# The third mixer with GpSimd's part given to TensorE, ScalarE and VectorE, and a run-time exchange of the fullest expert

## The chip, the core and the metric

The program runs on one core of one Trainium2 chip. The metric is the device time of one execution in microseconds: the median of three runs, and beside it one profiled execution with its trace. Engines: PE is TensorE (PEld its weight loads), DVE VectorE, ACT ScalarE, POOL GpSimd, SP SyncE, which issues most DMAs. Every engine takes its instructions in program order.

## What is computed

A batch of one with 256 positions of 1024 channels passes a first block (feed-forward layers, a short convolution, an mLSTM) and then a second block, with which the change deals:

```python
def second_block(...):
    h = layer_norm_2(x, ln_in_g, ln_in_b)          # right behind first_block's own last layer norm
    y = mixer_sublayer(h, ...)                     # the "third mixer"
    h = layer_norm_2(DEEPNORM_ALPHA_2 * h + y, ln1_g, ln1_b)
    e = (p @ ple_proj) * sigmoid(h @ ple_gate)
    m = moe_ffn(h, w_router, router_bias, exp_w_up, exp_w_down)   # 16 experts, 2 for each position
    return layer_norm_2(DEEPNORM_ALPHA_2 * h + m + e, ln2_g, ln2_b)

def mixer_sublayer(h, ...):
    u_pool, u_conv, c_q, c_kv, k_r, g_logits = split(h @ w_in)
    gates = sigmoid(g_logits + b_gate)
    y_pool = pool_mixer(u_pool) @ pool_proj        # causal mean over 2, 4, 8, 16 positions less u, then 4 small products
    y_conv = conv_module(u_conv) @ conv_proj       # depthwise convolution of width 31 on 512 channels, layer norm, silu
    y_mla = mla(c_q, c_kv, k_r) @ mla_proj         # 8 heads, softmax over allowed keys
    return (gates[0] * y_pool + gates[1] * y_conv + gates[2] * y_mla) @ w_out
```

Everything is float32. A weight matrix is used as a pair: `wh`, rounded to the fast matmul type fp32r, and `wl = raw - wh`; three matmuls (h·wh, l·wh, h·wl) stand for one product. A matmul on plain fp32 operands needs no pair.

## The kernel before

The 256 positions lie in two tiles t = 0, 1 of 128 partitions (`X_72`, `X_73` in the order listings below), or, transposed, channels on partitions and 256 positions along a row. `first()` runs the first block up to 1034 us; its instructions are the same after the change. `second()` follows:

- **Boundary.** While the last feed-forward's down products end (`g.tail`), DVE norms each tile twice: `ln_math` with the first block's gain and bias `gb`, then again with the second block's (`yp` in the listings). Each norm is statistics (L637, L639, L619), POOL's `rs_r` (L621), then four DVE operations on halves of 512 (L644 subtract mean and multiply gain, L645 multiply `rs_r` and add bias). TensorE turns the tile by transposes (L657), ACT rounds it to `xh` (L660), DVE makes `xl` (L664). `m2_head(t)` then projects tile t.
- **m2_body.** `conv_in` and the attention's input product, the pool products `pool_mm` (L1376), the attention's norms and transposes (`cTh`, `cTl`), queries (`uq`, L1312 turns them), keys, values. Then three merges in the order pool, attention, convolution (`MERGE`), each a gate product (L583 to L585), a projection, and DVE's multiply and add (L1578, L1580). Between a merge's blocks stand steps of the softmax (`mla`: scores L1420, exponent L1431, norm L1438 and L1440, turn L1455, output L1466) and of the convolution (`tap`).
- **pool_mean** runs on POOL: some 30 operations (L1393 to L1399) for the four windows; DVE splits the result into `yp` (L569).
- **conv31.** Channel groups 0 to 2 of four take 30 taps each on DVE (L1501 `cz`); group 3 takes 30 on ACT and POOL: ACT scales a shifted row into `tap` (L1493), POOL adds it (L1494). Tables (`TAPS_...`) say how many taps follow each block.
- **Weight pairs** of this part come through a ring (`st`): SP loads `raw`, ACT rounds it to `wh` (L298), and DVE or POOL makes `wl` (L299). Tables (`PUMP_...`) say which; POOL makes 21 between 1034 and 1340 us.
- **Routing** (1300 to 1345 us) is a chain of small DVE operations. It picks the fullest expert, and from it one run-time number, the row of its weights; 32 positions beyond an expert's 64 slots go through a spill round that needs the fullest expert's six weight tiles a second time (`SPILL`).
- **moe.** 16 experts in a fixed order (`_expert(i)`), six tiles of 1 MB each, in all 108 tiles with six for the spill round and six for gate and projection. SP issues the loads as slots come free; in the loop's last step (e = 15) the spill round runs beside expert 15. `combine` adds the results, `last_ln` norms and stores them.

Of the kernel before, what the change touches and what calls it, by code (L numbers as in the profile page):

```python
# [8 lines left out]
F32 = mybir.dt.float32  # L9
# [6 lines left out]
P = 128  # L16
# [29 lines left out]
def _pieces():  # L46
# [68 lines left out]
    def pl(j):  # L115
        add(("pl", j), 1024, "w_in_2", lambda w: _cols(w[0], j * P))
# [36 lines left out]
TAPS_POOL = "1011112302111112", "2020233020033323"  # L153
TAPS_MLA = "1111111010202032", "2300320331230300"
PUMP_POOL = "1210"
PUMP_MERGE = "13100221", "10112311", "10013123"
TAPS_CONV = "2020121032020130", "1030200011320012"
# [12 lines left out]
N_TILES = 108  # L170
SPILL = 16
# [4 lines left out]
def _wtile(e, j):  # L176
    e = 15 if e == SPILL else 16 if e == 15 else e
    return 6 * e + j + (6 if e >= GATE_AT else 3)


WTILES = {_wtile(e, j): (e, j) for e in range(17) for j in range(6)}
# [67 lines left out]
class Stream:  # L249
    def __init__(self, k, ws):  # L250
# [17 lines left out]
        self.raw, self.hl = {}, {}  # L268
# [21 lines left out]
    def split(self):  # L290
        i = self.nsplit
        r = self.slot(i)[0]
# [6 lines left out]
        self.eng.tensor_sub(l[:, :n], src, h[:, :n])  # L299
        self.hl[i] = (h, l)  # L300
        self.nsplit += 1

# [11 lines left out]
    def get(self, key):  # L314
        i = self.index[key]
        while self.nsplit <= i:
            assert self.slot(self.nsplit)[1] < self.free, key
            self.split()
# [35 lines left out]
def _const():  # L354
# [13 lines left out]
    return c  # L368

# [115 lines left out]
class Kernel:  # L485
# [142 lines left out]
    def ln_steps(self, t, accs, scale, eps, gb=None):  # L628
# [538 lines left out]

    def m2_open(self):
# [9 lines left out]
        self.cs = [x.rearrange("p a n -> p (a n)") for x in (self.tp, self.sg)]  # L1178

# [29 lines left out]
    def trig(self, p):  # L1209
        nc = self.nc  # L1210
        pi = p.tile([P, T], I32, name="pu0")
        pos = self.a["pos"]
        nc.gpsimd.dma_start(pi, bass.AP(tensor=pos.tensor, offset=pos.offset, ap=[[0, P], [1, T]]))
        ang = p.tile([P, T], F32, name="pu1")
        n = p.tile([P, T], F32, name="pu2")
# [13 lines left out]
    def m2_body(self):  # L1229
# [3 lines left out]
        self.qf = p0.tile([P, 8, T], F32, name="qf")  # L1233
        self.kf = p0.tile([P, 8, T], F32, name="kf")
        self.vv = [p0.tile([P, 512], F32, name=f"vv{t}") for t in range(2)]
# [4 lines left out]
        self.bcast(qg, a["rowp"][776:1416])  # L1240
        self.rot = p.tile([P, 2, T], F32, name="rot")
        self.cos, self.sin = self.rot[:, 0], self.rot[:, 1]
        self.trig(p)
# [15 lines left out]
        junk = p.tile([P, 384], F32, name="pm0")  # L1259
# [13 lines left out]
        next(cin, None)  # L1273
        self.taps = self.conv31()
        self.yp = self.m2.tile([P, 2, 4, T], F32R, name="yp")
        u = [self.pool_mm(p, j) for j in range(2)]
# [8 lines left out]
        u += [self.pool_mm(p, 2)]  # L1285
# [13 lines left out]
        u += [self.pool_mm(p, 3)]  # L1299
        for j in range(4):  # L1300
            self.pool_mean(p, j, u[j])
# [941 lines left out]
```

## Time and profile before

| | us |
|---|---|
| median of three runs (lowest, highest) | 1604.82 (1602.35, 1605.71) |
| the profiled execution's own time | 1610.17 |
| its span, first to last instruction | 1608.4 |
| PE busy | 1517.4 (94%) |
| DVE busy | 922.0 (57%) |
| ACT busy | 637.4 (40%) |
| POOL busy | 157.6 (10%) |

Busy shares are averages over stages that have different limits. Rows name a line of the kernel, an engine, an operation, and output<-input. A wait is the idle time of an engine ahead of an instruction, with what released it. The granted clock is the share of full speed that TensorE was given; 1.00 stands for 2.4 GHz.

### The profile page before, as it was taken

Reading aid. Unit: us, or ns where it says so; the run is one execution under the profiler, and the core shown is the slowest. Engines: PE = TensorE matmul, PEld = TensorE weight load, DVE = VectorE, ACT = ScalarE, POOL = GpSimd, SP = SyncE. Lnnn points to the kernel's source line nnn. Section 1 sums busy time; section 2 is a strip of 40 time slices with the busy share of each in tenths; the row PEclk is TensorE's granted clock in tenths of the full one; section 3 lists DMA queues with packets and bytes.
Section 4 is the critical chain, followed back from the end, with each engine's and each line's share of the span. In section 5 each row is a group of like instructions: output and inputs, shape, how many; then the busy total and the mean of one; then the engine's idle time right before and its main releaser. Section 6 shows DMA issues by size and latency. Waiting matters only on the chain.

```text
span 1608.4 us, 23409 instructions
## 1 busy us (share of the span) xinstructions
PE 1517.4 (94%) x9667; PEld 1249.1 (78%) x9668; DVE 922.0 (57%) x1367; ACT 637.4 (40%) x998; POOL 157.6 (10%) x161
## 2 busy tenths in 40 slices
PE   7999999899999999999999999979797999999986
PEld 5999989779999899988777999858687974434432
DVE  5654567575456755577667455577899564222223
ACT  4544435444443544435524444416663431111111
POOL 1000000000000000010000000133675200000001
PEclk9999999999999999999999999989898999999998
DMA  6655546354554654535325555325416666999993
GB/s 253 236 210 183 184 145 221 132 208 163 206 184 145 238 178 180 187 138 221 131 105 209 184 184 184 135 115 205 142 53 240 227 253 262 407 370 415 417 417 157
DMA packets 57391, 338.68 MB, mean 211 GB/s; under 512 B 6464, under 2 KB 6768, under 8 KB 25536
## 3 DMA queue, kind: packets, MB, share of 16 engines
q1 hardware_dynamic: 55008, 325.97, 54.0%
q0 software_dynamic: 1696, 8.96, 1.5%
q10 hardware_dynamic: 576, 2.22, 0.4%
q8 instruction: 77, 1.26, 0.3%
q14 instruction: 34, 0.28, 0.1%
HBM read 336.07 MB, written 1.05 MB: 210 GB/s over the span
## 4 chain that ended last, share of the span: by engine, by line
PE 73%; DVE 15%; issue 4%; DMA 3%; ACT 3%; POOL 1%; DVEq 0%; SPq 0%; ACTq 0%; POOLq 0%
PE mm L583 11%; PE mm L584 11%; PE mm L585 11%; PE mm L1914 7%; PE acc L573 6%; PE acc L574 6%; PE acc L575 6%; DVE wl L299 4%; PE mm L1937 3%; DVE cz L1501 3%; DMA raw<-in_ws_dram 2%; ACT wh L298 1%; DMA wh<-in_we_dram 1%; PE mm L1883 1%; DVE X L644 1%
## 5 line engine op out<-in xcount | busy, mean ns | idle before, releaser
L299 DVE TENSOR_TENSOR wl<-raw,wh 128x1024 fp32r<-128x1024 f32 (+1 forms) x381 | 458.8, 1244 | 117.9 <-ACT wh L298 117.8
L583 PE MATMUL mm<-xh,wh 128*128 128x256 f32 x1640 | 465.0, 284 | 0.0
L298 ACT CAST wh<-raw 128x1024 fp32r<-128x1024 f32 (+1 forms) x404 | 403.3, 1043 | 149.7 <-PE acc L575 57.5
L584 PE MATMUL mm<-xl,wh 128*128 128x256 f32 x1640 | 462.4, 282 | 0.0
L585 PE MATMUL mm<-xh,wl 128*128 128x256 f32 x1640 | 461.8, 282 | 0.0
L583 PEld LDWEIGHTS mm<-xh,wh 128*128 128x128 f32 x1640 | 311.5, 190 | 5.2 <-issue 2.7
L584 PEld LDWEIGHTS mm<-xl,wh 128*128 128x128 f32 x1640 | 310.9, 190 | 2.2
L585 PEld LDWEIGHTS mm<-xh,wl 128*128 128x128 f32 x1640 | 311.3, 190 | 0.0
L393 DVE TENSOR_TENSOR fm<-fs,mm 128x256 f32<-128x256 f32 x80 | 33.7, 422 | 209.5 <-ACT fs L391 209.5
L391 ACT ACTIVATE fs<-mm 128x256 f32<-128x256 f32 x80 | 30.8, 386 | 294.3 <-PE mm L585 294.3
L575 PE MATMUL acc<-wh,fhl 128*128 128x512 f32 x352 | 140.0, 398 | 4.9 <-DVE fhl L569 4.9
L573 PE MATMUL acc<-wh,fhh 128*128 128x512 f32 x352 | 141.1, 401 | 3.3 <-ACT fhh L568 3.3
L574 PE MATMUL acc<-wl,fhh 128*128 128x512 f32 x352 | 140.5, 399 | 0.0
L621 POOL TENSOR_TENSOR rs_r<-rs_v,nhalf 128x1 f32<-128x1 f32 (+2 forms) x22 | 18.3, 830 | 1102.3 <-DVE rs_v L619 1062.5
L575 PEld LDWEIGHTS acc<-wh,fhl 128*128 128x128 f32 x352 | 67.0, 190 | 22.7 <-DVE fhl L569 7.0
L573 PEld LDWEIGHTS acc<-wh,fhh 128*128 128x128 f32 x352 | 67.0, 190 | 18.3 <-ACT fhh L568 5.5
L574 PEld LDWEIGHTS acc<-wl,fhh 128*128 128x128 f32 x352 | 66.9, 190 | 12.6
L299 POOL TENSOR_TENSOR wl<-raw,wh 128x1024 fp32r<-128x1024 f32 (+1 forms) x23 | 58.8, 2567 | 69.0 <-ACT wh L298 69.0
L1501 DVE SCALAR_TENSOR_TENSOR cz<-cz,par 128x256 f32<-128x256 f32 x90 | 65.3, 787 | 0.0
L569 DVE TENSOR_TENSOR fhl<-fm,fhh 128x256 fp32r<-128x256 f32 x80 | 34.1, 426 | 37.8 <-ACT fhh L568 37.8
L1918 ACT ACTIVATE es<-mm 128x256 f32<-128x256 f32 x16 | 6.2, 384 | 117.8 <-PE mm L1914 117.8
L602 PE MATMUL mm<-wh,xh 128*128 128x512 f32 x128 | 45.3, 438 | 4.1 <-ACT xh L660 2.5
(574 smaller groups left out, 2147.6 us busy)
## 6 DMA issues: line engine op xcount, KB each, us to landing
raw<-in_ws_dram SPq DMA_DIRECT2D x197, 1024.0 KB, 4.9
wh<-in_we_dram SPq DMA_DIRECT2D x61, 512.0 KB, 11.3
wl<-in_we_dram SPq DMA_DIRECT2D x61, 512.0 KB, 11.3
w<-in_we_dram SPq DMA_DIRECT2D x23, 1024.0 KB, 12.3
raw<-in_we_dram SPq DMA_DIRECT2D x18, 1024.0 KB, 11.3
gb<-in_lnp_dram POOLq DMA_DIRECT2D x5, 1024.0 KB, 5.1
raw<-in_ws_dram SPq DMA_DIRECT2D x3, 768.0 KB, 4.9
w<-in_wg_dram SPq DMA_DIRECT2D x2, 1024.0 KB, 8.7
```

The source lines that it names most:

```text
L298: self.nc.scalar.copy(h[:, :n], src)
L299: self.eng.tensor_sub(l[:, :n], src, h[:, :n])
L573: mm(out, lh, rh, start=first, stop=False)
L574: mm(out, lh, rl, start=False, stop=False)
L575: mm(out, ll, rh, start=False, stop=last)
L583: mm(out, h[:, c], xh[:, k, s], start=k == 0, stop=False)
L584: mm(out, h[:, c], xl[:, k, s], start=False, stop=False)
L585: mm(out, l[:, c], xh[:, k, s], start=False, stop=k == kn - 1)
L602: mm(ps, self.xh[:, kk, s], h[:, c], start=kk == 0, stop=False)
L1501: nc.vector.scalar_tensor_tensor(o, cz[:, j, d:d + T], dw[j][:, d:d + 1], o, op0=OP.mult, op1=OP.add)
L1914: nc.tensor.matmul(ps[64 * b:64 * b + 64], x, w[:, c:c + 512], start=d == 0, stop=d == KT - 1)
L1937: self.nc.tensor.matmul((pb if i else pa)[64 * i:64 * i + 64], hT[:, a, 64 * b:64 * b + 64], w[:, c:c + 512], start=k == 0, stop=k == 3)
```

## The change

It changes seven things in `second()` and behind it. Line numbers below are the changed kernel's.

1. **Boundary.** The second norm no longer writes a finished tile on DVE. `ln_in` takes the statistics, and ACT normalises the tile in two operations of 512. `in_T` transposes that, and 16 ACT operations of 128x128 apply gain and bias, which lie along partitions now: 8 write `xh`, 8 write the same in fp32 (`y32`, buffer `cz`). `in_low` makes `xl` on DVE. `in_gain` applies gain and bias to the tile itself by four DVE operations of 128x1024, behind both heads.
2. **Weight pairs.** All `wl` are made on DVE but one at the boundary; the tables of POOL's share are gone.
3. **pool_mm and pool_mean.** The pool product is made with positions on partitions, 48 matmuls of 512 columns (before 96 of 256). The mean less u is a product with a constant band matrix: three fp32 matmuls (128, 16 and 128 columns) for each window. The matrix comes by one DMA.
4. **conv31.** Group 3: ACT scales the identity by one tap (128x128, `tap<-ident`), TensorE multiplies the shifted rows by that diagonal (fp32, 256 columns), four taps or six gathering in PSUM, and DVE adds the sum. 30 ACT operations, 30 matmuls, 8 DVE additions.
5. **Softmax.** A reciprocal on DVE and four ACT scalings in each of four steps replace POOL's power and products.
6. **The experts' order.** The fullest expert outside the four that are fixed at the front changes places with the last. The spill round uses the last expert's tiles, so its six own are gone (`N_TILES` 108 to 102). Twelve rows of weights are read by SP from `r_sel` at run time (before one), and routing has 15 more DVE operations (`swap` and others).
7. **The spill round's steps** in the last step move: down products of expert 14 first, spill's gate and up, transposes of 15, then behind the loop spill's transposes, down of 15, spill's down, the outputs.

```diff
 def second(self, g, acc, fs, fe):
-        self.slab_eng, self.slab_pumps, self.slab_ahead = nc.gpsimd, 4, 0
+        self.slab_eng, self.slab_pumps, self.slab_ahead = nc.vector, 4, 2
         self.ln_math(0, acc[0], fs, fe)
-        g.tail(range(NF - LAST2, NF - LAST2 + 2), "pp")
-        self.ln_math(0, None, 0, EPS, self.gb2)
-        g.tail(range(NF - LAST2 + 2, NF), "vpvp")
-        self.ln_pair((acc[1], fs, fe), [(None, 0, EPS, self.gb2)])
+        g.tail(range(NF - LAST2, NF - LAST2 + 2), "")
+        for _ in range(2):
+            st.cast()
+        self.ln_in(0)
+        st.low()
+        g.tail(range(NF - LAST2 + 2, NF), "")
...
+        ln = self.ln_steps(1, acc[1], fs, fe)
+        next(ln)
+        self.in_T(0)
+        next(ln)
+        self.in_low(0)
...
+        self.ln_in(1)
+        st.low()
         self.m2_head(0)
-        self.ln_T(1)
+        self.in_T(1)
+        self.in_low(1)
         self.m2_head(1)
+        self.in_gain()
         self.m2_body()
+    def ln_in(self, t):
...
+        for s in range(2):
+            xs = x[:, s * 512:(s + 1) * 512]
+            nc.scalar.activation(xs, xs, AF.Identity, scale=r, bias=mv[:, 0:1])
+    def in_T(self, t):
...
+        for y in (self.xh[:, :, t * P:(t + 1) * P], self.y32[:, t].rearrange("p (k n) -> p k n", k=KT)):
+            for k in range(KT):
+                nc.scalar.activation(y[:, k], pts[k // 4][:, k % 4 * P:(k % 4 + 1) * P], AF.Identity,
+                                     scale=g[:, k:k + 1], bias=b[:, k:k + 1])
+    def pool_mean(self, j, u):
...
+        mm(ps[:, P:T], u[1][:, c], b[:, BAND:], start=True, stop=False)
+        mm(ps[:, P:BAND], u[0][:, c], b[:, P:BAND], start=False, stop=False)
+        mm(ps[:, :P], u[0][:, c], b[:, :P], start=False, stop=True)
+        self.split(self.yp[:, 0, j], self.yp[:, 1, j], ps[:, :T])
 def norm(x):
-            nc.gpsimd.tensor_tensor(sm, sm, neg, op=OP.pow)
+            nc.vector.reciprocal(sm, sm)
             for b, g in enumerate(gs):
-                nc.gpsimd.tensor_tensor(pr[g], pr[g], sm[:, b, :, None].to_broadcast([P, n, P * (t + 1)]), op=OP.mult)
+                for i in range(n):
+                    nc.scalar.activation(pr[g][:, i], pr[g][:, i], AF.Identity, scale=sm[:, b, i:i + 1])
 def side():
-            for d in range(30):
-                tap = self.tp[:, d % 2]
-                nc.scalar.activation(tap, cz[:, 3, d:d + T], AF.Identity, scale=dw[3][:, d:d + 1])
-                nc.gpsimd.tensor_tensor(o, o, tap, op=OP.add)
+            for d0 in range(0, 30, 4):
+                n = min(4, 30 - d0)
+                for i in range(n):
+                    nc.scalar.activation(dg[:, i], self.ident, AF.Identity, scale=dw[3][:, d0 + i:d0 + i + 1])
                 yield
+                ps = self.acc()
+                for i in range(n):
+                    nc.tensor.matmul(ps[:, :T], dg[:, i], cz[:, 3, d0 + i:d0 + i + T], start=i == 0, stop=i == n - 1)
+                nc.vector.tensor_tensor(o, o, ps[:, :T], op=OP.add)
+                yield
-N_TILES = 108
-SPILL = 16
+N_TILES = 102
+FIXED = 4
+LAST_E = 7
 def wsrc(self, i):
-        if e < SPILL:
+        if e < FIXED:
             r = (6 * _expert(e) + j) * P
             return a["we"][r:r + P]
...
+        return a["we"][bass.ds(self.row * (6 * P) + j * P, P)]
```

Three places in the order of instructions, of the kernel before and of the changed one apart.

VectorE at the boundary, before: the first tile `X_72` from its first norm (gain and bias in `gb`) to the end of the second (in `yp`).

```order
L644 SCALAR_TENSOR_TENSOR X_72<-X_72,ln_mv,gb 128x512
L645 SCALAR_TENSOR_TENSOR X_72<-X_72,rs_r,gb 128x512
L637 BN_STATS ln_st<-X_72 128x6 x2
L639 BN_AGGR ln_mv<-ln_st 128x2
L619 TENSOR_SCALAR rs_v<-ln_mv 128x1
L644 SCALAR_TENSOR_TENSOR X_72<-X_72,ln_mv,yp 128x512
L645 SCALAR_TENSOR_TENSOR X_72<-X_72,rs_r,yp 128x512
L644 SCALAR_TENSOR_TENSOR X_72<-X_72,ln_mv,yp 128x512
L645 SCALAR_TENSOR_TENSOR X_72<-X_72,rs_r,yp 128x512
L299 TENSOR_TENSOR wl_10126<-raw,wh_10125 128x1024
```

VectorE at the same place, after.

```order
L666 SCALAR_TENSOR_TENSOR X_72<-X_72,ln_mv,gb 128x512
L667 SCALAR_TENSOR_TENSOR X_72<-X_72,rs_r,gb 128x512
L1195 BN_STATS ln_st<-X_72 128x6 x2
L1197 BN_AGGR ln_mv<-ln_st 128x2
L641 TENSOR_SCALAR rs_v<-ln_mv 128x1
L1199 SCALAR_TENSOR_TENSOR ln_mv<-ln_mv,rs_r 128x1
L305 TENSOR_TENSOR wl_10100<-raw,wh_10099 128x1024
L305 TENSOR_TENSOR wl_10103<-raw,wh_10102 128x1024
L657 SCALAR_TENSOR_TENSOR X_73<-acc,X_73 128x512 x2
```

The four operations of 512 behind the statistics have left DVE's queue; one small operation and two `wl` stand there, and the second tile's first norm comes sooner.

VectorE from the attention's queries to the first merge, before: `cz` are taps of the convolution's groups 0 to 2, `yp<-pu` splits POOL's means, `yp<-acc,par` the pool products.

```order
L299 TENSOR_TENSOR wl_10939<-raw,wh_10938 128x1024
L1501 SCALAR_TENSOR_TENSOR cz<-cz,par 128x256 x6
L569 TENSOR_TENSOR yp<-pu_10611,yp 128x256
L569 TENSOR_TENSOR yp<-pu_10649,yp 128x256
L569 TENSOR_TENSOR yp<-pu_10707,yp 128x256
L569 TENSOR_TENSOR yp<-krep_10753,yp 128x256
L299 TENSOR_TENSOR wl_11009<-raw,wh_11008 128x1024
L1501 SCALAR_TENSOR_TENSOR cz<-cz,par 128x256 x3
L1350 SCALAR_TENSOR_TENSOR yp<-acc,par,yp 128x256 x2
```

VectorE at the same place, after.

```order
L591 TENSOR_TENSOR yp<-acc,yp 128x256
L305 TENSOR_TENSOR wl_10900<-raw,wh_10899 128x1024
L305 TENSOR_TENSOR wl_10930<-raw,wh_10929 128x1024
L1572 SCALAR_TENSOR_TENSOR cz<-cz,par 128x256 x6
L305 TENSOR_TENSOR wl_10962<-raw,wh_10961 128x1024
L305 TENSOR_TENSOR wl_10991<-raw,wh_10990 128x1024
L1572 SCALAR_TENSOR_TENSOR cz<-cz,par 128x256 x3
L1565 TENSOR_TENSOR cz<-cz,acc 128x256
L1420 SCALAR_TENSOR_TENSOR yp<-acc,par,yp 128x256 x2
```

More `wl` stand in DVE's queue, the splits of the means come singly and earlier and from PSUM, and an addition `cz<-cz,acc` of the diagonals' sum is new.

VectorE at routing's end, before: `r_cnt` is what SP reads at run time, `xg` the first experts' gathered input.

```order
L1860 TENSOR_SCALAR r_cb<-r_cb 128x16
L1861 TENSOR_SCALAR r_cf<-r_cb 128x16
L1862 TENSOR_REDUCE r_cf<-r_cf 128x1
L1864 CAST r_cnt<-r_cf 1x18
L1886 COPY xg_12910<-mm_12901 128x512
L1886 COPY xg_12932<-mm_12923 128x512
```

VectorE at routing's end, after. The number that SP reads, `r_sel`, is made four instructions ahead of the first of these; `r_rv` and `r_wv` are the exchanged columns.

```order
L1974 TENSOR_TENSOR r_aff<-r_m_12860,r_oh 128x32
L1975 TENSOR_TENSOR r_rk<-r_rk,r_aff 128x32
L1976 COPY r_rk<-r_rv 128x2
L1971 TENSOR_TENSOR r_aff<-r_wt,r_oh 128x32
L1972 TENSOR_REDUCE r_wv<-r_aff 128x2
L1973 TENSOR_TENSOR r_m_12868<-r_wt,r_wv 128x2
L1974 TENSOR_TENSOR r_aff<-r_m_12868,r_oh 128x32
L1975 TENSOR_TENSOR r_wt<-r_wt,r_aff 128x32
L1976 COPY r_wt<-r_wv 128x2
L1964 TENSOR_SCALAR r_rv<-r_rv 128x2
L1998 COPY xg_12904<-mm_12895 128x512
L1998 COPY xg_12926<-mm_12917 128x512
```

Thirteen small operations (these ten and three ahead of them) stand between `r_sel` and the `xg` copies that stood right behind `r_cnt`; two more stand ahead of `r_sel`.

## Rows read from the trace of the kernel before

**Rows 1.** Windows: busy time (instructions) of each engine, granted clock, DMA share, GB/s.

```profile
1046.60:1085.00 38.40, 27.39 (x105) 21.39 (x106) 29.38 (x39) 6.01 (x9) 14.44 (x11) 0.82 0.30 114
1120.00:1255.00 135.00, 110.26 (x803) 105.04 (x801) 123.62 (x174) 74.92 (x143) 85.18 (x87) 0.89 0.41 145
1346.00:1564.00 218.00, 217.88 (x1090) 89.80 (x1086) 50.93 (x106) 32.78 (x58) 2.69 (x6) 1.00 0.99 399
```

**Rows 2.** TensorE's waits from 1034 to 1120 us: total, times, longest.

```profile
PE acc L657 <- DVE X L645: 11.1, 4, 4.3
PE acc L1289 <- DVE cTl L569: 1.6, 1, 1.6
```

**Rows 3.** TensorE's waits from 1120 to 1300 us.

```profile
PE acc L574 <- DVE yp L569: 5.6, 2, 4.1
PE acc L1420 <- ACT pr L1431: 4.8, 1, 4.8
PE acc L583 <- DVE sg L1578: 4.1, 1, 4.1
PE acc L1512 <- DVE cz L1501: 2.9, 1, 2.9
```

**Rows 4.** TensorE's timeline in the last expert: start, duration, instructions, idle before.

```profile
1568.43 1.26 PE L1914 MATMUL mm<-wh,xg 128*64 128x512 f32 x4 [4.55 <-DMA wh<-in_we_dram]
1573.86 0.44 PE L1926 MATMUL mm<-ident,es 128*128 128x128 f32 x2
```

**Rows 5.** POOL's timeline at the boundary.

```profile
1038.68 5.22 POOL L299 TENSOR_TENSOR wl<-raw,wh 128x1024 fp32r<-128x1024 f32 x2
```

**Rows 6.** VectorE's timeline there, beside POOL's split and behind it.

```profile
1038.74 2.89 DVE L645 SCALAR_TENSOR_TENSOR X<-X,rs_r,gb 128x512 f32<-128x512 f32 x1 [0.47 <-POOL rs_r L621]
1044.48 0.75 DVE L645 SCALAR_TENSOR_TENSOR X<-X,rs_r,gb 128x512 f32<-128x512 f32 x1
```

**Rows 7.** Groups of VectorE from 1120 to 1255 us: busy, mean ns, idle before.

```profile
L1501 DVE SCALAR_TENSOR_TENSOR cz<-cz,par 128x256 f32<-128x256 f32 x90 | 65.3, 787 | 0.0
L299 DVE TENSOR_TENSOR wl<-raw,wh 128x1024 fp32r<-128x1024 f32 x21 | 29.7, 1418 | 5.8 <-ACT wh L298 5.8
```

**Rows 8.** VectorE's splits from 1255 to 1294 us, POOL hardly at work, as a group.

```profile
L299 DVE TENSOR_TENSOR wl<-raw,wh 128x1024 fp32r<-128x1024 f32 x4 | 4.9, 1222 | 7.1 <-ACT wh L298 7.1
```

**Rows 9.** VectorE's taps, three each time, POOL idle and POOL at work.

```profile
1149.57 1.27 DVE L1501 SCALAR_TENSOR_TENSOR cz<-cz,par 128x256 f32<-128x256 f32 x3
1214.69 4.76 DVE L1501 SCALAR_TENSOR_TENSOR cz<-cz,par 128x256 f32<-128x256 f32 x3
```

**Rows 10.** TensorE's timeline at the boundary: transposes and the start of each head.

```profile
1050.84 1.11 PE L657 MATMUL acc<-ident,X 128*128 128x128 f32 x4 [4.34 <-DVE X L645]
1055.15 1.20 PE L602 MATMUL mm<-wh,xh 128*128 128x512 f32 x2
1069.25 0.66 PE L657 MATMUL acc<-ident,X 128*128 128x128 f32 x4 [1.44 <-DVE X L645]
1073.55 1.20 PE L602 MATMUL mm<-wh,xh 128*128 128x512 f32 x2
```

**Rows 11.** ScalarE's exponents of 128x128 from 1034 to 1300 us, as a group.

```profile
L1431 ACT ACTIVATE pr<-acc,mx 128x128 f32<-128x128 f32 x8 | 2.9, 365 | 2.8 <-DVE mx L1428 2.7
```

**Rows 12.** TensorE: eight fp32 matmuls of 256 columns (16 records).

```profile
1174.24 3.72 PE L1420 MATMUL acc<-kf,qf 128*128 128x256 f32 x16
```

**Rows 13.** POOL's splits from 1120 to 1255 us, as a group.

```profile
L299 POOL TENSOR_TENSOR wl<-raw,wh 128x1024 fp32r<-128x1024 f32 x10 | 25.0, 2508 | 27.0 <-ACT wh L298 27.0
```

**Rows 14.** VectorE at routing's end.

```profile
1342.96 0.17 DVE L1862 TENSOR_REDUCE r_cf<-r_cf 128x1 f32<-128x16 f32 x1
1343.17 0.17 DVE L1864 CAST r_cnt<-r_cf 1x18 int32<-1x18 f32 x1
1343.25 1.27 DVE L1886 COPY xg<-mm 128x512 f32<-128x512 f32 x2
```

**Rows 15.** TensorE's first expert.

```profile
1344.89 1.51 PE L1914 MATMUL mm<-w,xg 128*64 128x512 f32 x6
```

More of the change, by code (lines that the diff above doesn't have):

```diff
@@ L176, in _wtile @@
 def _wtile(e, j):
[L177 removed]
     return 6 * e + j + (6 if e >= GATE_AT else 3)
[L181 removed]
+WTILES = {_wtile(e, j): (e, j) for e in range(16) for j in range(6)}
 def _expert(i):
@@ L288, in load, with cast @@
             self.nload += 1
-    def split(self):
+    def cast(self):
         i = self.nsplit
+        assert self.slot(i)[1] < self.free
         r = self.slot(i)[0]
@@ L368, in _const, with _bands @@
     return c
+BAND = P + 16
+def _bands():
+    s, t = np.arange(T)[:, None], np.arange(T)[None]
+    out = []
+    for j in range(4):
+        w = 2 << j
+        b = ((s <= t) & (s > t - w)) / np.minimum(t + 1, w) - (s == t)
+        out += [b[:P, :BAND], b[P:, P:]]
+    return np.concatenate(out, 1).astype(np.float32)
 class FFN:
@@ L1298, in m2_body @@
         nc.vector.memset(self.sin[64:128], 1.0)
-        u += [self.pool_mm(p, 3)]
+        self.pool_mm(3)
+        u = []
+        for t in range(2):
+            u.append(self.cs[t])
+            nc.scalar.copy(u[t], self.po[t])
         for j in range(4):
-            self.pool_mean(p, j, u[j])
+            if j > 0:
+                self.pool_mean(j - 1, u)
             if j == KR_AT:
@@ L1330, in m2_body @@
         self.tap(int(TAPS_BODY[2]))
-        for j in range(4):
-            self.split(self.yp[:, 0, j], self.yp[:, 1, j], u[j][:, 16:])
         h, w = st.get(("ukv", 0))
@@ L1984, in moe @@
                 self.moe_free(GATE_TILES[2:] + PROJ_TILES[1:])
-            if e == 15:
-                next(spill)
             ps = self.mm()
@@ L1992, in moe @@
                 hT = self.expert_T(s)
-                if e == 15:
-                    next(spill)
                 if e % 2 and e > 2:
@@ L2023, in moe @@
                 self.nrest = nc.values_load(self.cnt[0:1, 16:17], min_val=0, max_val=8)
-            if e == 15:
-                next(spill)
             if e:
@@ L2033, in moe @@
                     self.bcast(gb[:, i * D:(i + 1) * D], row[i])
-        ps = [self.mm(), self.slot(3)]
+        next(spill)
+        ps = [self.mm(), self.mm()]
         self.expert_down(*ps, 15, hT2, range(4))
+        next(spill)
         self.expert_out(*ps, 15)
-        self.moe_free([_wtile(e, j) for e in (15, SPILL) for j in range(6)])
+        next(spill)
+        next(spill)
+        self.moe_free([_wtile(15, j) for j in range(6)])
         self.combine(7, True)
@@ L2221, in arrays @@
         "const": _const(),
+        "band": _bands(),
+        "lnc": np.concatenate([row("ln_in_" + n + "_2").reshape(KT, P).T for n in "gb"], 1),
         "lnp": np.stack([np.stack([f["ln_g"][l, j], f["ln_b"][l, j]]) for l in range(2) for j in range(3)] +
```

204 lines of the change are left out of this document (130 added, 74 removed).

## The prediction

> **What bounds the kernel now.** I read the windows by stage first. In the experts (1346 to 1564 us) TensorE is busy for 217.88 of 218 us and the DMA engines for 0.99: two limits lie on each other there. In the stretch from the queries to the convolution's norm (1120 to 1255 us) TensorE is busy for 110.26 of 135 us at a granted clock of 0.89; at the head of the second block (1046.6 to 1085 us) for 27.39 of 38.40 us at 0.82 [rows 1]. So the reader is to see two slack stretches, each paying twice: in waits, and in a clock that is lower where TensorE waits (in the experts, without waits, it is 1.00). Next I read TensorE's waits. Up to 1120 us nearly all are for the normalised tile, 11.1 us in four [rows 2]; from 1120 to 1300 us the largest are for pool's means, the softmax's exponents, a merge's sum and the convolution's rows [rows 3], and all but the exponents come from VectorE. In the last expert one wait of 4.55 us is for a weight tile [rows 4].
>
> VectorE is late because it shares time with POOL. While POOL makes two `wl` (5.22 us, from 1038.68) [rows 5], a multiply-add of 512 takes 2.89 us; behind them 0.75 us [rows 6]. The 90 taps take 65.3 us, 787 ns each [rows 7]; three take 1.27 us with POOL idle and 4.76 us with POOL at work [rows 9]. A split of its own takes 1.418 us there and 1.222 us in the next stretch, where POOL does little [rows 7, 8].
>
> **First block, no change.** The instructions up to 1034 us are the same.
>
> **Boundary and heads: −9 us.** TensorE's down products end at 1046.5 (1050.84 less the wait of 4.34); the first head's products run from 1055.15 to 1067.8 (1069.25 less 1.44), the second's from 1073.55 to about 1085 [rows 10]. In the change tile 0 is normalised sooner: POOL's two splits leave the first norm, so two operations go from 2.89 to 0.75 us (−4.3 [rows 6]), so the first norm ends near 1041 where it ended at 1045.2; statistics, POOL's `rs_r` and ACT's two operations of 512 (some 4 us, an estimate) bring the tile to 1045, ahead of TensorE's end. Transposes then take about 1.1 us (the row of 1.11 us for four, the second four beside ScalarE), and eight ACT operations of 128x128 write `xh`. No such operation is in the trace; the nearest is the exponent with a per-partition operand, 365 ns [rows 11], so 2.9 us, and the head starts near 1050.5 where it started at 1055.15. The other eight (`y32`) and `in_low` run beside its first 16 matmuls. It ends near 1062.5 with 12.7 us of work. Tile 1 has its own norm done by then; its transposes stand behind head 0 in TensorE's queue, so 1.1 + 2.9 us of wait remain, and the second head starts near 1066.5 and ends, after 11.3 us less some slow clock, near 1076. Bounds: −4 (ScalarE also has casts in that queue, and a ring slot for the third and fourth column group may be late by 2 us) and −12 (no wait for tile 1). `in_gain`, four operations of 128x1024, stands behind both heads, where nothing asks for X before 1294 us.
>
> **conv_in to the queries (1085 to 1120): −2 us.** The wait of 1.6 us for `cTl` [rows 2] should go, since VectorE is free of POOL; 48 products of 512 columns are as long as 96 of 256. Bounds −3 and 0.
>
> **Queries to the convolution's norm (1120 to 1255): −11 us.** TensorE's work at full clock is 110.26 × 0.89 = 98.1 us. Added: 30 fp32 matmuls of 256 columns at 3.72 / 8 = 0.465 us [rows 12] = 14.0 us, and four band products of 272 columns, 4 × 0.49 = 2.0 us; together 114.1 us. That is work on the path, bought against 135 − 110.3 = 24.7 us of waits and 12.2 us of slow clock. VectorE's work: 123.6 us, less 65.3 − 90 × 0.42 = 27.5 for the taps (0.42 is a third of 1.27 [rows 7, 9]), less 29.7 − 21 × 1.22 = 4.1 for its own splits [rows 7, 8], less some 8 for the other operations with two operands in SBUF (an estimate from the same stretching), plus ten splits from POOL [rows 13] at 1.22 = 12.2, plus eight additions of 0.42 = 3.4: about 100 us. ScalarE loses 30 taps and gains 30 diagonals and 16 scalings, all near 0.4 us, and stays near 75. So both fit under TensorE. Remaining waits: the softmax chain 3.5 of 4.8 us (its maxima, a table load and exponents stay; POOL's power and product become 16 scalings on ScalarE), and 3.5 for the rest and for diagonals that come late; slow clock in proportion to waits, 12.2 × 7 / 24.7 = 3.5. 114.1 + 7 + 3.5 = 124.6, so −10.4; with part of the diagonals hidden in the modelled end of a row (3.72 us is to the last end, the next start came earlier) −11. Bounds: no waits and full clock, −21; half of all waits and slow clock left, 114.1 + 18.4 = 132.5, −2.5.
>
> Here a rule stands beside the sum. With POOL at work VectorE's two-input operations stretched by a factor of 3.7 [rows 9]. The Trainium skill, SBUF — State Buffer, section "Who interferes with whom", says that VectorE's second port is GpSimd's and is held exclusively, the loser blocked fully. By that, ten splits moved to VectorE cost it 12.2 us and free it of up to the 25.0 us that they take on POOL [rows 13], while a count of instructions alone would call the move a load of 12.2 us. The trace agrees with the rule [rows 5, 6].
>
> **1255 to 1338 us: none.** TensorE runs without waits worth naming, and its instructions stay.
>
> **Routing: +2 us.** 15 small operations of 0.21 us start to start (1342.96 to 1343.17) are 3.1 us ahead of the `xg` copies [rows 14]. The copies end at 1344.5 and TensorE begins its first expert at 1344.89 behind earlier work [rows 15], so some 0.4 to 1 us are covered: +2, bounds +1 and +3. SP's first run-time row stands behind the loads of the four fixed experts, and those go out until after routing.
>
> **End of the experts: −6 us.** Six tiles of 1.05 MB less are 6.3 MB, at 399 GB/s [rows 1] 15.8 us of DMA, more than the wait. The wait of 4.55 us goes, and the 16 products behind it, which trickle in over 5.4 us (1568.43 to 1573.86 [rows 4]), take 16 × 0.25 = 4.0 us (0.25 is a sixth of 1.51 [rows 15]): −1.4. What is late next is TensorE itself. Bounds: −3, since the spill round's output steps now stand near the end and may show up to 3 us there, and −6.5.
>
> **Sum.** −9 − 2 − 11 + 2 − 6 = −26 us: the profiled execution from 1610.17 to about 1584, the median from 1604.82 to 1579, since the profile stands 5.35 us above the median.
>
> **Rivals.** (1) New waits take the place of the old ones between 1120 and 1255 us: 30 diagonals in 7 groups put ScalarE ahead of TensorE's in-order queue, and behind a late diagonal stands the merge. If waits and slow clock keep three quarters of their 36.9 us, the stretch is 142 − 135 = +7 and the sum is −8: 1597; at half, 1587. For it: TensorE is given 16 us that were hidden; against it: diagonals depend on nothing but weights and are issued a block ahead. I price it at 1590. (2) The exchange of experts gives nothing: DMA at 0.99 may be late earlier in the loop as well, or the spill round's tail eats the gain: −26 + 6 = −20, 1585. (3) Slower: VectorE becomes the bound, if what stretched its operations isn't POOL but something that stays. Then 123.6 + 10 × 1.42 + 8 × 0.42 = 141.2 us of VectorE and some 10 us in which it waits make 1120 to 1255 us +16, the boundary brings −4, routing with the later start +2, conv_in 0, the experts −3: +11, 1616. It decides from a stretch of 150 us (+15 cancels the rest). Against it: the same operations stand side by side with POOL on and off [rows 6, 9]. (4) The change doesn't do what it says: were the fullest expert one of the four fixed ones, a whole further round would run. Counted from the reference's inputs, one expert has 66 positions, the next 51, and it isn't a fixed one; the chance is under 0.01.
>
> **Chances.** Forecast (1566 to 1586) 0.60; rival 1 (1586 to 1602) 0.20; rival 2 0.10; rival 3 and the like 0.07; less than 1564 some 0.03. The range takes in the bounds of the two large terms and most of rival 1: 1563 to 1595. A measurement here tells 0.2%, about 3.2 us: faster 0.89, same 0.04, slower 0.07.
>
> **What would show it.** Right: taps at about 0.4 us in VectorE's groups; the first head's products at 1050 to 1051 us, the second's near 1066; 1120 to 1255 us of before done in about 124 us with TensorE's waits under 10 us and a clock above 0.93; no wait for a weight tile behind 1560 us; the first expert 2 us later in relation to the router. Wrong: waits for `tap` or for the band's sums in TensorE's list, ScalarE busy where TensorE waits, taps still at 0.7 us, or a wait at the final combine for the spill round.

## The result, and the profile after

The changed kernel takes 1580.25 us in the median (1579.06 to 1588.32) against 1604.54 us of the kernel before; the ratio is 0.986, 95% interval 0.983 to 0.990. Its profiled execution takes 1579.06 us with a span of 1577.3 us, where that of before had 1608.4 us. A median of 1579 us was forecast, with 1563 to 1595 us as the range.

Landmarks that both programs have divide the span. They are the first addition to the first tile on VectorE (`X_72<-acc`), the first product of the first head, the first query product, the broadcast of the convolution's norm (`acc<-ident,rs_r`), the router's counts (`mm<-r_o,tri`), the first expert's first product, the end of the last combine, and the last instruction. Each length is a difference of two start times in the timelines.

| stretch, us | before | after | difference | forecast |
|---|---|---|---|---|
| up to the first tile's addition | 1034.6 | 1029.6 | −5.0 | 0 |
| to the first head's product | 20.56 | 12.90 | −7.7 | |
| to the first query product | 64.86 | 63.28 | −1.6 | −11 with the row above |
| to the convolution's norm | 134.95 | 122.44 | −12.5 | −11 |
| to the router's counts | 81.31 | 79.69 | −1.6 | 0 |
| to the first expert | 8.62 | 10.37 | +1.8 | +2 |
| to the last combine's end | 249.81 | 245.40 | −4.4 | −6 |
| to the end | 13.73 | 13.61 | −0.1 | |

The first row has the same instructions in both. In the fourteen profiles of this case that length lies between 1027.4 and 1034.6 us, and the profile of before stood 5.35 us above its median, so I take the 5.0 us as scatter. From the first tile's addition on the difference is 547.7 − 573.8 = −26.1 us; −26 was forecast. Between the medians it is −24.3 us.

The windows of the changed kernel, from the first head to the queries and from there to the convolution's norm, answer to [rows 1]:

```profile
1042.50:1105.80 63.30, 57.19 (x271) 44.41 (x272) 48.39 (x75) 39.96 (x77) 5.83 (x9) 1.00 0.56 203
1105.80:1228.20 122.40, 114.65 (x885) 109.53 (x884) 97.30 (x196) 75.78 (x158) 3.90 (x7) 0.99 0.43 158
```

In the second TensorE has more work than before (114.65 us busy against 110.26) in a shorter time, the clock is 0.99 where it was 0.89, and VectorE is busy for 97.30 us where it was for 123.62, though it makes 30 pairs instead of 21. Its groups there, beside [rows 7]:

```profile
L1572 DVE SCALAR_TENSOR_TENSOR cz<-cz,par 128x256 f32<-128x256 f32 x90 | 37.6, 481 | 0.0
L305 DVE TENSOR_TENSOR wl<-raw,wh 128x1024 fp32r<-128x1024 f32 x30 | 36.5, 1223 | 12.2 <-ACT wh L297 12.2
```

The same 90 taps take 37.6 us instead of 65.3. At the boundary VectorE's operations that took 2.89 us [rows 6] are back at the short time, and the first head starts as ScalarE begins to write `xh` (timelines of VectorE, ScalarE and TensorE):

```profile
1033.75 0.75 DVE L667 SCALAR_TENSOR_TENSOR X<-X,rs_r,gb 128x512 f32<-128x512 f32 x1 [0.47 <-POOL rs_r L643]
1034.42 0.75 DVE L666 SCALAR_TENSOR_TENSOR X<-X,ln_mv,gb 128x512 f32<-128x512 f32 x1
1042.00 2.90 ACT L1215 ACTIVATE xh<-acc,lnc 128x128 fp32r<-128x128 f32 x8 [1.02 <-PE acc L1211]
1042.51 0.84 PE L624 MATMUL mm<-wh,xh 128*128 128x512 f32 x2
```

TensorE's waits, for [rows 2, 3]: the largest at the boundary and the heads, then those up to the convolution's norm, then those from the router on.

```profile
PE mm L627 <- DVE wl L305: 2.5, 1, 2.5
PE acc L1270 <- DVE tap L1265: 1.4, 1, 1.4
PE mm L622 <- DVE xl L1222: 1.3, 4, 0.4
...
PE acc L1484 <- ACT pr L1495: 4.4, 1, 4.4
PE acc L595 <- DVE cz L1565: 1.7, 1, 1.7
PE acc L1564 <- ACT pT L1520: 1.6, 1, 1.6
...
PE mm L2026 <- DVE xg L1998: 1.6, 1, 1.6
PE mm L2049 <- DVE X L2064: 1.2, 1, 1.2
```

Of the 24.7 us of waits between queries and norm 7.7 us are left (122.40 − 114.65), more than half of them the softmax's; 7 us were forecast. The 11.1 us for the normalised tile are gone, but 2.5 us for a pair, 1.4 us for `tap` and 1.3 us for `xl` stand there now. The tile that TensorE waited for in the last expert [rows 4] is in time; new are 1.6 us for the first `xg` behind the longer routing and 1.2 us for a PSUM slot that the last outputs still read.

So the sum was right, and the large stretches were near their forecasts. Whether the parts did it that were credited with it is another question, and the runs answer it otherwise.

### The profile page after: what moved, and what is told of

It is laid out like the page before. It is cut to its first block, busy times and chain, and to the rows that moved or that the text cites. A ratio compares the mean times of both kernels' runs of the same rounds, so it can differ in the third digit from the quotient of the medians.

```text
span 1577.3 us, 23657 instructions
## 1 busy us (share of the span) xinstructions
PE 1512.0 (96%) x9703; PEld 1242.7 (79%) x9704; DVE 889.5 (56%) x1412; ACT 650.1 (41%) x1044; POOL 48.0 (3%) x66
## 5 line engine op out<-in xcount | busy, mean ns | idle before, releaser
L305 DVE TENSOR_TENSOR wl<-raw,wh 128x1024 fp32r<-128x1024 f32 (+1 forms) x401 | 476.3, 1226 | 125.4 <-ACT wh L297 125.3
L605 PE MATMUL mm<-xh,wh 128*128 128x256 f32 x1608 | 455.4, 283 | 0.0
L606 PE MATMUL mm<-xl,wh 128*128 128x256 f32 x1608 | 452.8, 282 | 0.0
L607 PE MATMUL mm<-xh,wl 128*128 128x256 f32 x1608 | 452.2, 281 | 0.0
L605 PEld LDWEIGHTS mm<-xh,wh 128*128 128x128 f32 x1608 | 304.7, 190 | 5.2 <-issue 2.8
L606 PEld LDWEIGHTS mm<-xl,wh 128*128 128x128 f32 x1608 | 304.4, 189 | 2.2
L607 PEld LDWEIGHTS mm<-xh,wl 128*128 128x128 f32 x1608 | 304.8, 190 | 0.0
L596 PEld LDWEIGHTS acc<-wl,fhh 128*128 128x128 f32 x352 | 66.9, 190 | 12.7
L590 ACT CAST fhh<-fm 128x256 fp32r<-128x256 f32 x80 | 32.5, 406 | 39.0 <-DVE fm L415 39.0
L2031 DVE TENSOR_TENSOR es<-es,mm 128x256 f32<-128x256 f32 x16 | 6.7, 421 | 71.7 <-ACT es L2030 71.7
```

Source lines behind the costliest of these rows:

```text
L305: self.eng.tensor_sub(l, src, h)
L596: mm(out, lh, rl, start=False, stop=False)
L605: mm(out, h[:, c], xh[:, k, s], start=k == 0, stop=False)
L606: mm(out, h[:, c], xl[:, k, s], start=False, stop=False)
L607: mm(out, l[:, c], xh[:, k, s], start=False, stop=k == kn - 1)
```

## The experiments

Lengths are of the same landmarks; "rest" is from the first tile's addition to the last instruction, which leaves the first block's scatter out.

| kernel | median us | to head | to queries | to norm | to first expert from counts | experts | rest |
|---|---|---|---|---|---|---|---|
| before | 1604.54 | 20.56 | 64.86 | 134.95 | 8.62 | 249.81 | 573.8 |
| after | 1580.25 | 12.90 | 63.28 | 122.44 | 10.37 | 245.40 | 547.7 |
| e1_no_trade | 1584.05 | 12.90 | 63.17 | 122.46 | 8.64 | 251.10 | 551.7 |
| e2_pool_taps | 1579.31 | 12.89 | 64.85 | 122.55 | 10.35 | 245.37 | 549.0 |
| e3_pool_splits | 1584.38 | 12.88 | 66.86 | 124.52 | 10.36 | 245.39 | 553.0 |
| e4_old_norm_pool | 1585.24 | 20.54 | 63.29 | 122.74 | 10.38 | 245.41 | 555.4 |
| e5_old_norm_dve | 1577.33 | 14.02 | 60.49 | 122.47 | 10.36 | 245.43 | 545.9 |
| e6_pool_reads | 1588.28 | 12.90 | 66.15 | 127.72 | 10.36 | 247.12 | 557.2 |
| e7_pool_memsets | 1580.20 | 12.89 | 64.66 | 122.70 | 10.37 | 245.44 | 549.0 |
| e8_before_dve_splits | 1581.93 | 14.03 | 60.54 | 125.24 | 8.63 | 251.18 | 553.1 |
| e9_old_pool_mean | 1583.26 | 12.89 | 64.46 | 125.62 | 10.36 | 245.42 | 551.7 |
| e10_old_softmax_norm | 1575.95 | 12.90 | 64.55 | 121.66 | 10.37 | 245.42 | 547.8 |
| e11_old_norm_late_swap | 1574.96 | 14.01 | 60.49 | 122.45 | 8.67 | 243.13 | 541.9 |
| e12_before_splits_exchange | 1578.57 | 14.02 | 60.35 | 125.62 | 8.66 | 243.14 | 544.7 |

A length is reproducible to 0.1 or 0.2 us where the instructions are the same, but for one: "to queries" is 63.2 or 64.6 in kernels that are alike there. The cause is the granted clock at the first head (windows of the changed kernel, then of e10_old_softmax_norm): 1.00 or 0.90 over the same 17.4 us.

```profile
1042.50:1060.00 17.50, 14.24 (x58) 9.83 (x59) 13.02 (x20) 13.42 (x27) 4.60 (x7) 1.00 0.55 175
```

```profile
1042.60:1060.00 17.40, 14.23 (x51) 10.17 (x52) 13.04 (x20) 11.99 (x24) 4.62 (x7) 0.90 0.55 173
```

So 1.4 us in that column, and in "rest", say nothing.

### The exchange of experts

The parts of the diff on the experts' order, routing and the last step are undone:

```diff
-N_TILES = 102
-FIXED = 4
-LAST_E = 7
+N_TILES = 108
+SPILL = 16
...
```

> The changed kernel with the exchange of experts and the moved spill steps undone (108 tiles, the fullest expert's six loaded a second time, routing and the last step as before). My theory: the exchange is worth 4.0 us of the stretch from the first expert's product to the last combine (249.4 us before, 245.4 after) and costs 1.8 us in routing. So a wait of 3 to 5 us for a weight tile comes back in the last expert, the stretch is 249 us, the step from the router's counts to the first expert is 8.6 us instead of 10.4, and the time is 1582 to 1583 us. Rival (the end is set by TensorE and the output steps alone, and the wait of before came from a late start): no wait for a tile, the stretch stays at 245 to 246 us, 1578 to 1579 us.

Measured: 1584.05 us; routing 1.7 us shorter, the experts 5.7 us longer. TensorE's largest wait from the router on:

```profile
PE mm L2006 <- DMA wh<-in_we_dram: 5.7, 1, 5.7
```

The exchange with the moved last step is worth 5.7 us, not 4.0, and costs 1.7. The experts take 251.1 us here and 249.8 in the kernel before, with the same tiles, since the wait is 5.7 instead of 4.55 us [rows 4]. A shorter lead of the DMA engines is not the reason: SyncE issues 26 loads of expert weights ahead of the first expert's product in both kernels, the first pair 70.8 us ahead in both (timelines). Why the last tile comes 1.2 us later stays open. The theory held, its size was low; the rival (no wait) fell.

### The diagonals

Group 3 of the convolution goes back to rows scaled on ScalarE and added on GpSimd, in the places that the tables of before give them:

```diff
-                    nc.scalar.activation(dg[:, i], self.ident, AF.Identity, scale=dw[3][:, d0 + i:d0 + i + 1])
...
-                    nc.tensor.matmul(ps[:, :T], dg[:, i], cz[:, 3, d0 + i:d0 + i + T], start=i == 0, stop=i == n - 1)
...
+                nc.scalar.activation(tap, cz[:, 3, d:d + T], AF.Identity, scale=dw[3][:, d:d + 1])
+                nc.gpsimd.tensor_tensor(o, o, tap, op=OP.add)
```

> The changed kernel with the convolution's fourth channel group taken on ScalarE and GpSimd again (30 scaled rows, 30 additions on GpSimd) instead of 30 diagonals, 30 fp32 matmuls and 8 additions on VectorE; all else as changed. My theory: TensorE loses 14 us of work between the queries and the convolution's norm, but GpSimd's 30 additions (28 us) stretch VectorE's taps from about 0.42 to 0.5 to 0.6 us, and VectorE's waits eat the 14 us; the stretch (122.4 us after, 135 before) stays between 119 and 128 us, 1577 to 1586 us. Rival 1 (the diagonals are only a cost on the path): the stretch is 108 to 110 us, 1567 us. Rival 2 (GpSimd's additions were the main harm): over 130 us, 1588 us or more.

Measured: the stretch is 122.55 us, with diagonals 122.44; 1579.31 us in the median. The window of the stretch, VectorE's taps and TensorE's two largest waits:

```profile
1109.00:1231.60 122.60, 105.22 (x826) 100.33 (x824) 105.31 (x188) 79.01 (x159) 31.95 (x37) 0.94 0.44 157
```

```profile
L1566 DVE SCALAR_TENSOR_TENSOR cz<-cz,par 128x256 f32<-128x256 f32 x90 | 47.7, 589 | 0.0
```

```profile
PE acc L1484 <- ACT pr L1495: 6.3, 1, 6.3
PE acc L1577 <- DVE cz L1566: 5.9, 1, 5.9
```

TensorE is busy for 9.4 us less (105.22 against 114.65). All of it comes back as waits, 17.4 us instead of 7.7, most of them for the taps, the exponents and the turned rows; the products are 14.0 us at full clock [rows 12], and busy time falls by less since the clock is 0.94 instead of 0.99. The diagonals buy waits for work one to one: no gain and no loss.

### The splits on GpSimd again

The pairs of the pool products and merges go by the tables of before:

```diff
-        st.pump(2)
+        st.pumps(PUMP_POOL[j])
...
-                st.pump(2)
+                st.pumps(PUMP_MERGE[MERGE.index(x)][i])
```

> The changed kernel with the weight pairs of the pool products and of the three merges given to GpSimd by the tables of before (18 or so of the splits), all else as changed. My theory, two engines that lock each other out: VectorE loses some 18 x 1.22 = 22 us of work but its taps stretch beside 45 us of GpSimd's splits, so VectorE's busy time between the queries and the convolution's norm rises from 97 us to 105 to 120 us, and the time by 3 to 10 us, 1583 to 1590 us. Rival (work is work, a split on an idle engine is free): VectorE's busy time falls to about 80 us, no change or a gain, 1575 to 1580 us.

Measured: 1584.38 us; 3.6 us longer to the queries (at a clock of 0.97 instead of 1.00), 2.1 to the norm. The window, the taps, and GpSimd's splits:

```profile
1109.10:1233.60 124.50, 116.06 (x885) 110.79 (x883) 103.99 (x187) 76.47 (x159) 27.54 (x16) 0.97 0.43 155
```

```profile
L1574 DVE SCALAR_TENSOR_TENSOR cz<-cz,par 128x256 f32<-128x256 f32 x90 | 45.5, 569 | 0.0
```

```profile
L307 POOL TENSOR_TENSOR wl<-raw,wh 128x1024 fp32r<-128x1024 f32 x9 | 23.8, 2641 | 96.4 <-ACT wh L299 43.8 <-PE acc L1566 41.2 <-DVE wl L307 5.8
```

VectorE makes nine pairs less (some 11 us) and yet is busy for 103.99 us instead of 97.30, just under the 105 us at which my theory began. The rival, a split on an idle engine is free, falls.

### The boundary in two steps

First the whole boundary as before, GpSimd's splits with it; then the same with every split on VectorE:

```diff
-        self.slab_eng, self.slab_pumps, self.slab_ahead = nc.gpsimd, 4, 0
+        self.slab_eng, self.slab_pumps, self.slab_ahead = nc.vector, 4, 0
         self.ln_math(0, acc[0], fs, fe)
-        g.tail(range(NF - LAST2, NF - LAST2 + 2), "pp")
+        g.tail(range(NF - LAST2, NF - LAST2 + 2), "vv")
         self.ln_math(0, None, 0, EPS, self.gb2)
-        g.tail(range(NF - LAST2 + 2, NF), "vpvp")
+        g.tail(range(NF - LAST2 + 2, NF), "vvvv")
```

> The changed kernel with the boundary as before: both norms of a tile on VectorE, four operations of 512 each, four of the boundary's splits and the heads' on GpSimd. My theory: the first head starts 8 us later behind TensorE's tail than in the changed kernel and the second ends 7 to 9 us later (50.2 us from the first tile's addition, against 42.4), the rest is the same: 1587 to 1589 us. Rival (the later stages were as much set free by the boundary's weights being ready, or they swallow the delay): 1580 to 1584 us.

> The changed kernel with the boundary's norms on VectorE as before, but with all splits of the boundary on VectorE too, so that GpSimd does nothing beside them. It divides the 7.7 us by which the first head starts sooner (12.9 us behind the first tile's addition, 20.6 with the old boundary) between GpSimd's share and the moved norm. My theory: without GpSimd the two stretched operations of each norm shrink (8.5 us of stretching for a tile), but two splits stand in VectorE's queue ahead of the second norm (2.4 us) and the four operations of 512 stay (3 us): the first head starts at 15 to 17 us, so some 4.5 us come from GpSimd's leaving and some 3 us from ScalarE's norm; time 1582 to 1585 us. Rival (the norm on ScalarE is the whole gain): 19 to 21 us, 1586 us or more. Rival 2 (GpSimd's leaving is all): 12.5 to 13.5 us, 1579 us.

Measured: 20.54 us to the first head with GpSimd, 14.02 without, 12.90 with the norm on ScalarE. Up to the queries together: 83.8, 74.5, 76.2 us. So GpSimd's leaving is worth 9.3 us, and the norm on ScalarE costs 1.7 us: it starts the head 1.1 us sooner and then loses 2.8. The clock over the first 17.4 us of the first head was 0.90 in the kernel without GpSimd and 1.00 in the changed one, so at like clocks the loss would be larger, some 3 us (an estimate: 1.7 + 1.4). In the old norm without GpSimd TensorE's largest wait there is

```profile
PE mm L622 <- DVE xl L687: 3.6, 1, 3.6
```

while the changed kernel waits 2.5 us for a pair that stands behind others in VectorE's queue, 1.4 us behind `in_gain`, and 1.3 us for `xl`. Neither theory gave this; I had expected 4.5 us from GpSimd and 3 us from ScalarE, and the rival that GpSimd's leaving is all came nearer. The first kernel's stretches came as expected (7.6 us later at the queries), but its median, 1585.24 us, is under the 1587 us that I had named. The second's, 1577.33 us, is below the changed kernel's.

### Splits on VectorE alone, in the kernel before

```diff
-PUMP_POOL = "1210"
-PUMP_MERGE = "13100221", "10112311", "10013123"
+PUMP_POOL = "0000"
+PUMP_MERGE = "00000000", "00000000", "00000000"
```

and the boundary as in the second step above.

> The kernel before with one thing changed: all splits of the weight pairs on VectorE, none on GpSimd. GpSimd keeps pool's means, the taps' additions and the softmax's products. My theory, GpSimd's splits lock VectorE for longer than they cost it: the first head starts 4 us sooner (16 instead of 20.6 us), and the stretch to the convolution's norm is shorter by 2 to 6 us; time 1594 to 1599 us. Rival (VectorE, busy for 124 of 135 us there, takes 12 us more and becomes the bound): 1610 us or more.

Measured: 1581.93 us, ratio 0.987 (0.986 to 0.989). The window from the queries to the norm, and the taps there:

```profile
1103.00:1228.20 125.20, 105.66 (x802) 100.96 (x800) 114.58 (x184) 72.88 (x142) 65.89 (x78) 0.90 0.43 155
```

```profile
L1501 DVE SCALAR_TENSOR_TENSOR cz<-cz,par 128x256 f32<-128x256 f32 x90 | 54.5, 664 | 0.0
```

This one part gives 573.8 − 553.1 = 20.7 of the 26.1 us: 6.5 to the head, 4.3 to the queries, 9.7 to the norm. VectorE has nine more pairs in the stretch (30 instead of 21) and 9 us less busy time than in the kernel before. I had expected 5 to 10 us; the sign of the theory was right, its size was half.

### Pool's means and the softmax's scaling as before

```diff
-        self.split(self.yp[:, 0, j], self.yp[:, 1, j], ps[:, :T])
...
+            nc.gpsimd.tensor_tensor(dst[:, 16:], src[:, 16:], src[:, 16 - d:16 + T - d], op=OP.add)
```

> The changed kernel with pool's means on GpSimd as before (96 products of 256 columns, some 30 operations on GpSimd, four splits of the result in one row on VectorE), all else as changed. My theory: GpSimd's 17 us stand at the start of the stretch, VectorE's splits of the means wait for the last of them, and TensorE waits for them ahead of the pool product, as in the kernel before (5.6 us); TensorE saves 2 us of band products: the stretch from the queries to the convolution's norm 125 to 130 us instead of 122.4, time 1583 to 1588 us. Rival (the means were hidden by other work once VectorE is free): 120 to 122 us, 1578 us.

```diff
-            nc.vector.reciprocal(sm, sm)
+            nc.gpsimd.tensor_tensor(sm, sm, neg, op=OP.pow)
```

> The changed kernel with the softmax's scaling on GpSimd as before (power and two products for each of the four steps), all else as changed. My theory: the wait for the exponents stays (4.4 us after, 4.8 before), since both ways stand behind the same maxima and exponents; GpSimd's 12 us of work stretch VectorE's taps a little: the stretch 122 to 125 us, 1580 to 1583 us. Rival (the 16 scalings on ScalarE hold up the other casts there, so that the old way is the better one): 119 to 121 us, 1577 us.

Measured: with the old means 125.62 us to the norm, 3.2 more, and 1583.26 us; a wait for the convolution's sum is the largest there (1.7 us in the changed kernel), not the one for the means:

```profile
PE acc L595 <- DVE cz L1563: 4.6, 1, 4.6
```

VectorE is busy for 101.6 us there instead of 97.30, so I read it thus: the means cost VectorE's queue time, and what stands behind is late. The wait that I had named did not come. With the old scaling the stretch is 121.66 us, 0.8 less, and the rest 547.8 against 547.7 us, with the 1.4 us of slow clock above in it. Its median, 1575.95 us, is 4.3 us under the changed kernel's and below what I had named for either theory, but the intervals against the kernel before (0.982 to 0.985 and 0.983 to 0.990) overlap. That the 16 scalings cost something (the rival) is likelier than that they gain, and not shown.

### GpSimd's load by itself

Two loads that no engine waits for are put into the changed kernel:

```diff
+        scr = self.m2.tile([P, 160], F32, name="scr")
+        for _ in range(90):
+            nc.gpsimd.tensor_tensor(scr, self.X[0][:, 0:160], self.X[1][:, 0:160], op=OP.add)
```

and, in the other, 250 times `nc.gpsimd.memset(scr, 0.0)`.

> The changed kernel with 90 additions on GpSimd (128x160, both inputs in SBUF) that nobody waits for, from the queries on; the result goes to a scratch tile, and nothing else changes. It puts back GpSimd's load alone. My theory, the two engines lock each other out while both read two SBUF operands: taps and splits on VectorE that fall beside the additions take 1.3 to 3 times as long, VectorE's busy time between the queries and the convolution's norm rises from 97 us to 110 to 140 us, and the stretch from 122.4 to 127 to 145 us. Rival (what harmed was that other engines waited for GpSimd's results): no operation is longer, 122 to 123 us, 1580 us.

> The changed kernel with 250 memsets on GpSimd (128x160) at the same place, which only write. My theory (the shared reading is what hurts): VectorE's taps stay at 0.48 us in the mean, the stretch at 122 to 124 us, 1579 to 1582 us. Rival (any work on GpSimd, or its writes, hurts VectorE): taps and stretch as with the additions.

Measured, taps on VectorE and the load on GpSimd, of the additions:

```profile
L1575 DVE SCALAR_TENSOR_TENSOR cz<-cz,par 128x256 f32<-128x256 f32 x90 | 46.1, 573 | 0.0
```

```profile
L1372 POOL TENSOR_TENSOR scr<-X,X 128x160 f32<-128x160 f32 x90 | 63.8, 709 | 7.0
```

and of the memsets:

```profile
L1575 DVE SCALAR_TENSOR_TENSOR cz<-cz,par 128x256 f32<-128x256 f32 x90 | 37.5, 478 | 0.0
```

```profile
L1372 POOL MEMSET scr<- 128x160 f32 x250 | 57.9, 232 | 14.3
```

With the additions the stretch is 5.3 us longer, VectorE is busy for 109.4 us in it instead of 97.30, and the time is 1588.28 us; with nearly as many microseconds of memsets 122.70 us and 1580.20 us, as without. Both of the additions' figures lie at the low end of what I had expected or just under it (110 to 140 us busy, 127 to 145 us for the stretch). Another 1.7 us of the additions' kernel lie in the experts, where GpSimd has nothing to do: the clock is 0.99 there instead of 1.00. Nobody waits for either result. What hurts VectorE is GpSimd's additions, which read two operands from SBUF, not its being at work, and not that its results come late. An operation with one input was not tried.

### A version from the runs

The changed kernel with the old norm on VectorE, the columns' exchange behind the first gather, and the last down products in one PSUM slot:

```diff
-        self.swap(rk, self.rv)
-        self.swap(wt, self.wv)
...
         xg = self.gather_quad(0)
+        self.swap(self.rk, self.rv)
+        self.swap(self.wt, self.wv)
...
-        ps = [self.mm(), self.mm()]
+        ps = self.mm()
```

> A version made from what the runs showed: the changed kernel with the old norm on VectorE (all splits on VectorE), the exchange of the columns (13 small operations) moved behind the first gather, and the last expert's down products in one PSUM slot instead of two. My theory: 1.7 us from the boundary (the stretch to the queries 74.5 instead of 76.2 us, as with the old norm), 1.8 us from the first expert's start (8.6 instead of 10.4 us behind the counts), and about 1 us from the wait of 1.22 us at the last down products: 1573 to 1577 us, against 1579 to 1580 us of the changed kernel. Rival (the experts are bound by DMA, so a sooner start is waited off at the end): the stretch of the experts grows by 1.8 us, 1576 to 1579 us.

> The kernel before with two parts of the change alone: all splits on VectorE, and the exchange of experts (with the columns' exchange behind the first gather and one PSUM slot for the last down products). GpSimd keeps pool's means, the taps' additions and the softmax's products. It asks what band, diagonals and ScalarE's scalings are worth together beside these two. My theory, from the single runs: the stretch to the convolution's norm is 125 us instead of 122.5, all else as in the kernel with the old norm and the late exchange, so 2 to 4 us slower than that one, 1576 to 1580 us. Rival (the parts need each other: with GpSimd wholly idle VectorE gains more than the sum): 1581 us or more.

Measured: 1574.96 us (ratio 0.982, 0.980 to 0.984), 5.8 us less than the changed kernel from the first tile's addition on: 1.7 at the boundary, 1.7 in routing, 2.3 in the experts. The waits of 1.6 and 1.2 us are gone, and the last down products take 3.6 us with one PSUM slot where they took 5.9 with two (timelines), which is the whole 2.3. The experts don't give the earlier start back, so the rival fell. The second kernel, which has parts 2, 6 and 7 of the seven, is 3.2 us slower to the norm and within 0.3 us elsewhere (544.7 against 541.9 us in all; 1578.57 us in the median).

## Why the prediction was right, and where its steps were not

**What bounds the kernel.** Right. VectorE, stretched by GpSimd, was what TensorE waited for; the two loads on GpSimd show the cause by itself.

**Boundary and heads, −9, and to the queries, −2.** Measured −9.3 together, where −11 was forecast. The step that failed is who earns it. The prediction took 4.3 us for GpSimd's two splits out of the first norm and gave the rest to ScalarE's norm, without asking what the old norm would take with GpSimd gone. That is 74.5 us against 76.2: the norm on ScalarE loses 1.7 us. The chain's pieces were also mis-sized. It put the first head 4.0 us behind TensorE's tail, and it starts 1.0 us behind it, since a product needs only the first of the eight written pieces. Its end was added up wrongly: 1050.5 + 12.7 is 1063.2, not 1062.5. And the bound of 2 us for a late ring slot came as 2.5 us for a late pair, for another reason: in the changed kernel's trace ScalarE's casts end at 1050.5 us, but the split begins at 1053.44 us, behind the second tile's statistics in VectorE's queue.

**Queries to the convolution's norm, −11.** Measured −12.5, and the terms are close: TensorE's work at full clock 114.65 × 0.99 = 113.5 us against 114.1, waits 7.7 against 7, slow clock about 1 against 3.5, VectorE's work 97.3 against 100, though a tap takes 0.48 and not 0.42 us. The working did not say what the parts are worth, and the runs give an uneven answer: the splits some 10 us, pool's means 3, diagonals and scalings nothing. Of the 16 us that were "bought against waits" the diagonals' 14 us bought waits at par. So rival 1 (new work and waits in the place of old ones) holds for the diagonals alone, and not for the stretch.

**The rule.** The Trainium skill, SBUF — State Buffer, section "Who interferes with whom", says that a VectorE instruction with two SBUF inputs contends with a GpSimd instruction that reads SBUF, not with one that only writes it. The two loads agree: 90 taps take 46.1 us beside the additions and 37.5 us beside the memsets. What the prediction drew from the rule, that a split which leaves GpSimd gives VectorE more than it costs, the runs show twice: VectorE's busy time falls by 9 us with nine pairs more (kernel before with the splits moved), and rises by 6.7 us with nine less (changed kernel with the splits moved back).

**1255 to the counts, none.** Measured −1.6. The instructions do stay; the clock was 0.98 in this stretch of the kernel before and is 1.00 now, as it is in the kernel before with the splits moved (79.77 us):

```profile
1255.00:1336.30 81.30, 79.39 (x493) 67.68 (x493) 47.68 (x98) 28.06 (x50) 9.71 (x6) 0.98 0.64 238
1228.20:1307.90 79.70, 77.80 (x494) 66.09 (x492) 48.00 (x101) 29.78 (x51) 2.34 (x3) 1.00 0.65 244
```

The prediction had no term for the clock here.

**Routing, +2; the end, −6.** +1.8 and −4.4. The wait went as said, and undoing the exchange costs 5.7 us, so rival 2 fell. The 16 products behind it were read wrongly: they did not trickle in but ran at a slow clock, and TensorE did not wait between them.

```profile
1568.40:1573.90 5.50, 5.45 (x17) 1.33 (x17) 0.00 (x0) 0.00 (x0) 0.00 (x0) 0.69 1.02 419
```

The 1.4 us came in even so, since the clock is 1.00 in the changed kernel's experts; for this piece that is luck. What is missing is the last down products in two PSUM slots of the reordered last step, 2.3 us more than in one, inside the bound of 3 us that was named for the step: in the version from the runs, with one slot, the stretch is 243.13 us, −6.7.

**Rival 3, slower.** Its mechanism (something that stays stretches VectorE) is refuted: the taps take 481 ns instead of 787.

## What to carry to other kernels

In this case an elementwise operation with two operands in SBUF was not free on an idle GpSimd while VectorE worked on such operations too. So read the same VectorE instruction beside GpSimd and alone, and if it stretches, move GpSimd's work before anything else; here that one edit brought four fifths of the gain. Where a change has several parts that lean on one cause, ask of each what it is worth with the others in place: the sum came out right with the credit in the wrong places. Work given to the engine that waits is worth no more than the waits that it replaces. And before two lengths are compared, compare their clocks: one slow spell was worth 1.4 to 1.7 us here, as much as some of the parts.

## What the runs showed of the hardware

GpSimd's additions and its memsets differ in what they do to VectorE: 64 us of additions from SBUF stretch 90 taps from 37.6 to 46.1 us, 58 us of memsets leave them at 37.5 us. And in this program a matmul waits for the slice that it reads, not for the whole tile: the first head starts 0.5 us behind the start of a group of eight ScalarE operations that takes 2.9 us.
